# Sixteen products of the recurrence and a modulation part's products moved to GpSimd

## The chip, the cores and the metric

The kernel runs on one core of one Trainium2 chip. The metric is the device time of one execution in microseconds (us); lower is better. A core has five engines that work side by side: TensorE (PE in the profile), VectorE (DVE), ScalarE (ACT), GpSimd (POOL) and SyncE (SP, which here only issues DMAs). Each engine works through its own list of instructions in a fixed order, and an instruction that waits holds up everything behind it in that list.

## The reference

One decoder block over 512 positions of 1024 features, in fp32. What matters here:

```python
# six vectors of modulation, from the condition c
mod = silu(c) @ w_ada + b_ada            # shift1, scale1, gate1, shift2, scale2, gate2
h = rms_norm(x) * (1 + scale1) + shift1
xr, gr, q, k, v, gm = split(h @ w_in)
# branch A: recurrence
log_a = -8 * r * softplus(-lam);  a = exp(log_a)      # r, i: sigmoid gates of conv(xr)
u = sqrt(-expm1(2 * log_a)) * (i * xr)
hs_t = a_t * hs_(t-1) + u_t                            # along the positions
y_rnn = hs * gelu(gr)
# branch B: differential attention of q, k, v -> y_attn
x = x + gate1 * ((gate_a * (y_rnn @ w_proj_rnn) + gate_b * (y_attn @ w_proj_attn)) @ w_out)
h2 = rms_norm(x) * (1 + scale2) + shift2
out = x + gate2 * (relu(h2 @ w_ff1) ** 2 @ w_ff2)
```

## The kernel before

Activations lie with the features on 128 partitions and the 512 positions along a row: eight tiles of 128x512 make one 512x1024 matrix. Every matmul of a weight is done three times in a reduced fp32 format (`mm3`): the weight `w` is split into a high part `wh` (ScalarE, line 122) and a rest `wl` (VectorE, line 123), the activation likewise into a pair. So one 128x1024 weight unit costs a DMA of 512 KB, a cast on ScalarE, a subtraction on VectorE, and 24 matmuls of 512 columns. The loaded tiles `w` have three buffers in one pool, the pairs `wh`/`wl` two.

The program is written as one long list; a scheduler sorts it at build time into a fixed order for each engine. Around the change there are two places.

**The recurrence beside the first attention heads.** For each of the eight tiles n: `lru_sqrt` (a square root on ScalarE, line 453, then a product `xc<-xc,th` on VectorE, line 455), `lru_scan` (an exponential on ScalarE, line 460, then on VectorE line 461 and the scan of line 462), and `y_rnn` (product with the gate `gel` on VectorE, line 471; cast to `yh` on ScalarE, line 473; rest `yl` on VectorE, line 143). All these work in place in the tile `xc`. The string `PLAN` sets where the eight scans s0 to s7 stand between matmuls of the merge gates (`gm`) and of q and k (`qk`), and `heads()` interleaves them with the attention of the first two heads: scores `sc` (TensorE, line 582), their minimum and mask (VectorE, line 587, tile `e`), exponential (ScalarE, line 589), combination of the two maps (VectorE, line 596), transposes `aT` (TensorE, line 604), copies `aTs` (ScalarE line 607 or VectorE line 609), products with v, `po` (TensorE, line 615). When a head is done, `head_norm` scales its output `o` (VectorE, line 635) and `head_out` transposes it, `yT` (TensorE, line 642).

**The last modulation part (gate2).** It is a product of a 1024x1024 matrix with one vector, done by rows in eight pieces of 128x1024: load `ada` (a tile of the same pool and tag as the weights, three buffers), and one VectorE instruction (line 188) that multiplies by the vector `cb` and sums along the row. The eight pieces stand in the hidden-layer loops of the second and third quarter of the feed-forward net, after tiles n = 4 to 7 of each; each loop step also loads a weight of `w_ff1` (24 matmuls `f`), and applies relu and square on ScalarE (lines 865 and 876).

```python
if qd in (1, 2) and n >= 4:
    ada_chunk(5, 4 * (qd - 1) + n - 4)
```

Of the kernel before, what the change touches and what calls it, by code (L numbers as in the profile page):

```python
# [16 lines left out]
F32 = mybir.dt.float32  # L17
# [3 lines left out]
AF = mybir.ActivationFunctionType  # L21
ALU = mybir.AluOpType
AX = mybir.AxisListType

P = 128
S = 512
D = 1024
# [26 lines left out]
def build(tc, out, x, xT_in, c, pos, vecs, reps, ada, w_xr, w_xr7, w_qk, w_v, w_gr, w_gm, w_lru,  # L54
          w_pr, w_pa, w_out, w_ff1, w_ff2):
    nc = tc.nc
    from contextlib import ExitStack

    with ExitStack() as es:
        const = es.enter_context(tc.tile_pool(name="const", bufs=1))  # L60
        wpool = es.enter_context(tc.tile_pool(name="w", bufs=3))
# [9 lines left out]
        def slot(tag, bufs, name, dt=F32):  # L71
            return (big if tag in "mh" else mix).tile([P, S], dt, name=name, tag=tag, bufs=bufs)

        def t_(name, dt=F32, tag="t"):
            return (tmp if tag == "t" else mix).tile([P, S], dt, name=name, tag=tag,
                                                     bufs=dict(t=B_T, a=B_A, r=B_R)[tag])

        def tiny(name, n, dt=F32):
            return tmp.tile([P, n], dt, name=name, tag=f"s{n}", bufs=4 if n >= 32 else 12)
# [22 lines left out]
        def after(later, earlier):  # L102

            tc.add_manual_dep(later.ins, earlier.ins.name,
                              mybir.DependencyInfo(mybir.DependencyClass.NoSync, mybir.DependencyReason.DATA),
                              reason="activation tables")
# [35 lines left out]
        def split_l(dst, src, h):  # L142
            return nc.vector.tensor_tensor(dst, src, f32(h), op=ALU.subtract)
# [24 lines left out]
        cb = const.tile([P, D], F32, name="cb")  # L168
# [8 lines left out]
        bada = const.tile([P, 48], F32, name="bada")  # L177
# [4 lines left out]
        mod = const.tile([P, 48], F32, name="mod")  # L182

        def ada_chunk(j, k):
            col = j * 8 + k
            w = wpool.tile([P, D], F32, name=f"ada{col}", tag="w", bufs=3)
            nc.sync.dma_start(w, ada[j, k])
            nc.vector.tensor_tensor_reduce(w, w, cb, 1.0, bada[:, col:col + 1], op0=ALU.mult,  # L188
                                           op1=ALU.add, accum_out=mod[:, col:col + 1])

        def ada_halves(j, k, prev=None):

            col = j * 8 + k
            start = bada[:, col:col + 1]
            for i in range(2):
                w = slot("q", B_Q, f"ada{col}_{i}")
                cols = slice(i * S, (i + 1) * S)
                nc.sync.dma_start(w, ada[j, k][:, cols])
                end = mod[:, col:col + 1] if i else tiny(f"adah{col}", 1)
                i_ = nc.vector.tensor_tensor_reduce(w, w, cb[:, cols], 1.0, start, op0=ALU.mult,  # L200
                                                    op1=ALU.add, accum_out=end)
                start = end
                if prev is not None:
                    after(i_, prev)
# [247 lines left out]
        def lru_sqrt(n, u, th, prev):  # L452
            i = nc.scalar.activation(th, th, AF.Sqrt)
            after(i, prev)
            nc.vector.tensor_tensor(u, u, th, op=ALU.mult)
            return i

        def lru_scan(n, a, u, prev):
# [9 lines left out]
            return g, nc.scalar.activation(g, ps, AF.Gelu_apprx_tanh)  # L468

        def y_rnn(n, hs, g):  # L470
            nc.vector.tensor_tensor(hs, hs, g, op=ALU.mult)
            yh = slot("y", B_Y, f"yh{n}", F32R)
            nc.scalar.copy(yh, hs)
            yl = slot("y", B_Y, f"yl{n}", F32R)
            split_l(yl, hs, yh)
            return yh, yl
# [190 lines left out]
        for n in range(KC):  # L667
# [6 lines left out]
            if n == QT0:  # L674
                qk0 = qk_transpose(0, qk0)
        v0 = run(gv)
        sqs = [lru_sqrt(n, lg[n][1], lg[n][2], lg[-1][3]) for n in range(KC)]
        y_att = [None] * NH
        th0, m0, th1 = [], [], []
# [16 lines left out]
        def fill():  # L696

            rot = {}
            for group in PLAN.split("/"):
                for op in group.split():  # L700
                    o, n = op[0], int(op[1:])
                    if o == "g":
                        gate0(n)
                    elif o == "s":
                        hs = lru_scan(n, lg[n][0], lg[n][1], sqs[-1])
                        yr.append(y_rnn(n, hs, gel[n][0]))
                    elif o == "q":
                        rot[n] = yield from qk_quarter(n)
                    elif o == "t":
                        qks[n] = qk_transpose(n, rot.pop(n))  # L710
                    elif o == "v":
                        vs[n] = yield from v_half(n)
                    elif o == "p":
                        proj_rnn(n)
                    elif o == "m":
                        th1.append(gate(KC + n, slot("y", B_Y, f"thg{KC + n}")))
                if o not in "qv":
                    yield
# [49 lines left out]
        for n in range(KC):  # L768
            pp = project(w_pa[n], y_att, f"pa{n}")
            ada_chunk(3, n)  # L770
            th = t_(f"mg{n}")
            nc.vector.scalar_tensor_tensor(th, th1[n], 1.0, pp, op0=ALU.add, op1=ALU.mult)
            nc.vector.tensor_tensor(th, th, m0[n], op=ALU.add)
            mh = slot("y", B_Y, f"mh{n}", F32R)
            nc.scalar.copy(mh, th)
            ml = slot("q", B_Q, f"ml{n}", F32R)
            split_l(ml, th, mh)
            mg.append((mh, ml))
# [80 lines left out]
        def hidden_relu(qd, n, dst):  # L859
            if qd == 0 and n < NU:  # L860
                nc.vector.tensor_tensor(dst, early[n], rb2, op=ALU.mult)
                nc.scalar.activation(dst, dst, AF.Relu, bias=shw[:, n:n + 1])
            else:
                ps = project(w_ff1[qd, n], h2, f"f1_{qd}_{n}")
                nc.scalar.activation(dst, ps, AF.Relu)

        def hidden(qd, ahead):

            raw = [ff.tile([P, 4, S], F32, name=f"r2_{qd}_{c}", tag="raw", bufs=2) for c in range(2)]
            for n in range(KC):  # L870
                rl = raw[n // 4][:, n % 4, :]
                if n < len(ahead):
                    nc.scalar.activation(rl, ahead[n], AF.Square)
                else:
                    hidden_relu(qd, n, rl)
                    nc.scalar.activation(rl, rl, AF.Square)
                if qd in (1, 2) and n >= 4:
                    ada_chunk(5, 4 * (qd - 1) + n - 4)
            return raw

        def out_product(qd, raw, beside):
# [178 lines left out]
        for qd in range(4):  # L1060
            raw = hidden(qd, ahead)
            ahead = []

            def beside():

                if qd < 3:
                    ahead.append(t_(f"ahead{qd + 1}_{len(ahead)}"))
                    hidden_relu(qd + 1, len(ahead) - 1, ahead[-1])

            beside()  # L1070
            out_product(qd, raw, beside)
# [66 lines left out]
```

## Time and profile before

| | |
|---|---|
| median of 3 runs | 877.34 us (877.32 to 877.82) |
| the profiled execution's own time | 876.41 us |
| its span, first to last instruction | 874.6 us |
| TensorE busy | 861.0 us, 98% |
| VectorE busy | 651.5 us, 74% |
| ScalarE busy | 449.2 us, 51% |
| GpSimd busy | 15.1 us, 2% |
| granted TensorE clock | full in all 40 slices |

The span is 1.8 us shorter than the time of the execution it comes from, and that execution was 0.9 us below the median. "Busy" counts the time in which an engine has an instruction in work. Matmuls are pipelined and their recorded ends are modelled: two matmuls of 512 columns that follow each other start some 0.23 us apart, though each is listed with 0.39 us. So what TensorE loses is seen from the starts.

### The profile page before, as it was taken

The page shows a single profiled execution, that of the slowest core. Times are in us where ns is not written, and L with a number is a line of the kernel's source. Part 1 is how long each engine was busy: PE and PEld are TensorE (multiplying, and loading weights), DVE is VectorE, ACT ScalarE, POOL GpSimd, SP SyncE. Part 2 cuts the span into 40 slices and gives each one's busy share as a digit, 9 for nine tenths or more (in the row PEclk, how much of TensorE's full clock was granted, in tenths as well). Part 3 has the DMA queues.
Part 4 walks back from the last instruction along what each step waited for, and adds up shares of the span by engine and source line. Part 5 has one row for each costly group of instructions (what it writes and reads, how often), then busy time and mean ns, then how long its engine had stood idle before and what let it go on. Part 6 is the DMA issues. An engine that isn't in the chain of part 4 may idle for free.

```text
span 874.6 us, 11292 instructions
## 1 busy us (share of the span) xinstructions
PE 861.0 (98%) x4012; PEld 705.5 (81%) x4012; DVE 651.5 (74%) x1251; ACT 449.2 (51%) x748; POOL 15.1 (2%) x50
## 2 busy tenths in 40 slices
PE   6999999999999999999999999999999999999998
PEld 3888887877878888888888888888888888888887
DVE  6997995599859855786758556858766885876397
ACT  6673547985536543535623343747545544554461
POOL 1000000000000000000000000000000000002110
PEclk9999999999999999999999999999999999999999
DMA  8979425412255372238336332822641344139572
GB/s 315 370 250 319 152 97 134 136 68 73 87 131 169 99 191 76 93 87 227 110 126 210 132 121 75 273 87 72 193 148 70 128 161 169 49 126 235 120 122 96
DMA packets 64572, 128.92 MB, mean 147 GB/s; under 512 B 6146, under 2 KB 30850, under 8 KB 64516
## 3 DMA queue, kind: packets, MB, share of 16 engines
q1 hardware_dynamic: 59236, 122.97, 43.3%
q0 software_dynamic: 5280, 5.24, 3.9%
q8 instruction: 31, 0.51, 0.2%
q14 instruction: 25, 0.20, 0.1%
HBM read 113.51 MB, written 2.10 MB: 132 GB/s over the span
## 4 chain that ended last, share of the span: by engine, by line
PE 86%; DVE 10%; DMA 1%; issue 1%; ACT 1%; SPq 1%; ACTq 0%; DVEq 0%
PE f L131 6%; PE f L129 6%; PE f L130 6%; PE X L131 3%; PE X L130 3%; PE X L129 3%; PE gm L129 3%; PE gm L130 3%; PE gm L131 3%; DVE wl L123 2%; PE sc L582 2%; PE qk L131 2%; PE qk L129 2%; PE qk L130 2%; PE xr L129 2%; PE pr L129 2%
## 5 line engine op out<-in xcount | busy, mean ns | idle before, releaser
L122 ACT CAST wh<-w 128x1024 fp32r<-128x1024 f32 (+1 forms) x113 | 118.0, 1044 | 214.5 <-issue 48.1
L123 DVE TENSOR_TENSOR wl<-w,wh 128x1024 fp32r<-128x1024 f32 (+1 forms) x113 | 137.0, 1213 | 68.1 <-ACT wh L122 64.5
L131 PE MATMUL f<-h2h,wl 128*128 128x512 f32 x240 | 93.5, 390 | 0.4 <-DVE wl L123 0.4
L130 PE MATMUL f<-h2l,wh 128*128 128x512 f32 x240 | 93.2, 389 | 0.0
L129 PE MATMUL f<-h2h,wh 128*128 128x512 f32 x240 | 92.9, 390 | 0.0
L131 PEld LDWEIGHTS f<-h2h,wl 128*128 128x128 f32 x240 | 45.0, 188 | 10.1 <-DVE wl L123 0.8
L130 PEld LDWEIGHTS f<-h2l,wh 128*128 128x128 f32 x240 | 45.1, 188 | 9.4
L129 PEld LDWEIGHTS f<-h2h,wh 128*128 128x128 f32 x240 | 45.0, 188 | 9.3
L130 PE MATMUL gm<-hl,wh 128*128 128x512 f32 x128 | 51.0, 398 | 0.0
L129 PE MATMUL qk<-wh,hh 128*128 128x512 f32 x128 | 50.7, 396 | 0.0
L129 PE MATMUL gm<-hh,wh 128*128 128x512 f32 x128 | 50.5, 394 | 0.0
L131 PE MATMUL gm<-hh,wl 128*128 128x512 f32 x128 | 50.5, 394 | 0.0
L131 PE MATMUL qk<-wh,hl 128*128 128x512 f32 x128 | 50.4, 394 | 0.0
L130 PE MATMUL qk<-wl,hh 128*128 128x512 f32 x128 | 50.4, 394 | 0.0
L941 DVE TENSOR_TENSOR p_1l<-b,p_1h 128x1024 fp32r<-128x1024 f32 x24 | 29.4, 1223 | 26.3 <-ACT p_1h L940 26.1
L589 ACT ACTIVATE e<-e,nm 128x128 f32<-128x128 f32 (+3 forms) x64 | 35.7, 559 | 24.4 <-DVE nm L587 24.4
L940 ACT CAST p_1h<-b 128x1024 fp32r<-128x1024 f32 x24 | 25.2, 1051 | 31.0 <-PE f L130 22.9
L941 DVE TENSOR_TENSOR p_0l<-b,p_0h 128x1024 fp32r<-128x1024 f32 x24 | 29.3, 1223 | 15.0 <-ACT p_0h L940 13.8
L587 DVE CUSTOM_DVE_ANT_0 e<-sc,mask 128x128 f32<-128x128 f32 (+3 forms) x64 | 30.3, 484 | 9.9 <-PE sc L582 9.9
L940 ACT CAST p_0h<-b 128x1024 fp32r<-128x1024 f32 x24 | 25.3, 1055 | 24.2 <-PE X L131 12.4
L188 DVE CUSTOM_DVE_ANT_0 ada<-ada,cb,bada 128x1024 f32<-128x1024 f32 x16 | 20.5, 1283 | 14.3 <-DMA ada<-in_ada 14.1
L984 DVE TENSOR_TENSOR b<-b,b 128x1024 f32<-128x1024 f32 x24 | 29.1, 1220 | 0.1
(444 smaller groups left out, 2216.9 us busy)
## 6 DMA issues: line engine op xcount, KB each, us to landing
ada<-in_ada SPq DMA_DIRECT2D x64, 256.0 KB, 5.8
w<-in_w_ff SPq DMA_DIRECT2D x32, 512.0 KB, 3.2
b<-in_w_ff SPq DMA_DIRECT2D x30, 512.0 KB, 3.4
w<-in_w_qk SPq DMA_DIRECT2D x16, 512.0 KB, 3.2
w<-in_w_gm SPq DMA_DIRECT2D x16, 512.0 KB, 3.7
ada<-in_ada SPq DMA_DIRECT2D x16, 512.0 KB, 3.3
b_t<-in_w_ff POOLq DMA_DIRECT2D x10, 512.0 KB, 6.5
w<-in_w_gr SPq DMA_DIRECT2D x8, 512.0 KB, 4.0
```

Of the source, the lines that this page charges most:

```text
L122: i_w = nc.scalar.copy(wh[:, :n], w[:, :n])
L123: nc.vector.tensor_tensor(wl[:, :n], w[:, :n], f32(wh)[:, :n], op=ALU.subtract)
L129: nc.tensor.matmul(ps, lh, rh, start=first, stop=False, skip_group_check=more)
L130: nc.tensor.matmul(ps, lh, rl, start=False, stop=False, skip_group_check=more)
L131: nc.tensor.matmul(ps, ll, rh, start=False, stop=last, skip_group_check=more)
L188: nc.vector.tensor_tensor_reduce(w, w, cb, 1.0, bada[:, col:col + 1], op0=ALU.mult, op1=ALU.add, accum_out=mod[:, col:col + 1])
L582: nc.tensor.matmul(ps[m][:, :nn], q[m][:, qc], k[m][r][:, :nn], start=r == 0, stop=r == 1)
L587: nc.vector.tensor_tensor_reduce(e[:, :n], ps[m][:, :n], mask[:, S - n:], 1.0, 1e30, op0=ALU.add, op1=ALU.min, accum_out=nm)
L589: nc.scalar.activation(e[:, :n], e[:, :n], AF.Exp, bias=nm, scale=-1.0, accum_out=sums[:, m:m + 1])
L940: nc.scalar.copy(v4(wh), v)
L941: nc.vector.tensor_tensor(v4(wl), v, f32(v4(wh)), op=ALU.subtract)
L984: nc.vector.tensor_tensor(d, d, s_, op=ALU.add)
```

## The change

`lru_sqrt` and `y_rnn` issue their products on GpSimd instead of VectorE: 8 + 8 instructions of 128x512. The eight pieces of the last modulation part go through a new function: GpSimd multiplies (128x1024), ScalarE copies the product onto itself and sums it along the row, VectorE adds the bias to that one column. What is computed stays the same. Lines below 188 move down by 10 in the new kernel (471 becomes 481).

```diff
+        def ada_beside(j, k):
+
+            col = j * 8 + k
+            w = wpool.tile([P, D], F32, name=f"ada{col}", tag="w", bufs=3)
+            nc.sync.dma_start(w, ada[j, k])
+            nc.gpsimd.tensor_tensor(w, w, cb, op=ALU.mult)
+            sm = tiny(f"adas{col}", 1)
+            nc.scalar.activation(w, w, AF.Copy, accum_out=sm)
+            nc.vector.tensor_tensor(mod[:, col:col + 1], sm, bada[:, col:col + 1], op=ALU.add)
...
         def lru_sqrt(n, u, th, prev):
             i = nc.scalar.activation(th, th, AF.Sqrt)
             after(i, prev)
-            nc.vector.tensor_tensor(u, u, th, op=ALU.mult)
+            nc.gpsimd.tensor_tensor(u, u, th, op=ALU.mult)
             return i
...
         def y_rnn(n, hs, g):
-            nc.vector.tensor_tensor(hs, hs, g, op=ALU.mult)
+            nc.gpsimd.tensor_tensor(hs, hs, g, op=ALU.mult)
             yh = slot("y", B_Y, f"yh{n}", F32R)
             nc.scalar.copy(yh, hs)
...
                 if qd in (1, 2) and n >= 4:
-                    ada_chunk(5, 4 * (qd - 1) + n - 4)
+                    ada_beside(5, 4 * (qd - 1) + n - 4)
```

The scheduler sorts all engines anew. TensorE has the same rows; its order differs in the stretch of the first two heads. There, first before and then after, stand the rows around the transpose `yT` of head 0's output `o` (the `qk` are matmuls of q and k, `sc_3` the scores of head 1's last block of rows, `aT_1` a transpose of its second):

```order
L131 MATMUL qk_3_2105<-wh_2172,hl_298 128x512
L129 MATMUL qk_3_2105<-wh_2172,hh_346 128x512
L130 MATMUL qk_3_2105<-wl_2173,hh_346 128x512
L131 MATMUL qk_3_2105<-wh_2172,hl_350 128x512
L582 MATMUL sc_3_0_2203<-kh_3_0_1509,qs_1_0_1494 128x512
L582 MATMUL sc_3_0_2203<-kl_3_0_1512,qs_1_0_1494 128x512
L582 MATMUL sc_3_1_2204<-kh_3_1_1515,qs_1_1_1497 128x512
L582 MATMUL sc_3_1_2204<-kl_3_1_1518,qs_1_1_1497 128x512
L129 MATMUL qk_0_2102<-wh_2229,hh_398 128x512
L642 MATMUL yT_2156<-ident,o_2015 128x128 x4
```

```order
L131 MATMUL qk_3_2105<-wh_2172,hl_298 128x512
L652 MATMUL yT_2156<-ident,o_2015 128x128 x4
L129 MATMUL qk_3_2105<-wh_2172,hh_346 128x512
L130 MATMUL qk_3_2105<-wl_2173,hh_346 128x512
L131 MATMUL qk_3_2105<-wh_2172,hl_350 128x512
L592 MATMUL sc_3_0_2203<-kh_3_0_1509,qs_1_0_1494 128x512
L592 MATMUL sc_3_0_2203<-kl_3_0_1512,qs_1_0_1494 128x512
L592 MATMUL sc_3_1_2204<-kh_3_1_1515,qs_1_1_1497 128x512
L592 MATMUL sc_3_1_2204<-kl_3_1_1518,qs_1_1_1497 128x512
L129 MATMUL qk_0_2102<-wh_2229,hh_398 128x512
L614 MATMUL aT_1_2165<-ident,e_1_0_2087 128x128 x2
```

The transposes `yT` now stand eight matmuls of 512 columns further ahead.

On VectorE, at the same place, the rows that end with `o`, first before and then after (`xc_1247`, `xc_1292` and `xc_1337` are tiles 5, 6 and 7 of the recurrence, the `or` columns the scale of `o`, `cc` a column of the softmax; the scans, line 462, are listed with the name of their sibling instruction):

```order
L462 SCALAR_TENSOR_TENSOR xc_1247<-r_1650,xc_1247 128x512
L98 SCALAR_TENSOR_TENSOR or0b_2045<-or0a_2043,or0v 128x4
L461 SCALAR_TENSOR_TENSOR xc_1292<-r_1699,xc_1292 128x512
L99 SCALAR_TENSOR_TENSOR or_2026<-or0b_2045,or0y_2040 128x4
L593 RECIPROCAL rr_2050<-sm_2_2137 128x2
L471 TENSOR_TENSOR xc_1247<-xc_1247,gel_1245 128x512
L633 TENSOR_TENSOR or_2026<-or_2026,rr_1749 128x4
L595 SCALAR_TENSOR_TENSOR cc_2_2153<-sm_2_2137,nlam,rr_2050 128x1
L635 TENSOR_TENSOR o_2015<-o_2015,or_2026 128x512
```

```order
L98 SCALAR_TENSOR_TENSOR or0b_2045<-or0a_2043,or0v 128x4
L472 SCALAR_TENSOR_TENSOR xc_1337<-r_1718,xc_1337 128x512
L99 SCALAR_TENSOR_TENSOR or_2026<-or0b_2045,or0y_2040 128x4
L603 RECIPROCAL rr_2050<-sm_2_2137 128x2
L643 TENSOR_TENSOR or_2026<-or_2026,rr_1749 128x4
L605 SCALAR_TENSOR_TENSOR cc_2_2153<-sm_2_2137,nlam,rr_2050 128x1
L645 TENSOR_TENSOR o_2015<-o_2015,or_2026 128x512
```

The products of line 471 are gone (six of them stood ahead of `o`), and the scans of tiles 6 and 7 and line 461 of tile 7, which came after `o`, now come ahead of it.

On ScalarE, in the hidden loop of the second quarter, the rows from the relu of tile 3, first before and then after (`wh` are the casts of the weights of the next tiles, `adas` the sums of the modulation):

```order
L865 ACTIVATE r_1_0_6209<-f_1_3_6220 128x512
L876 ACTIVATE r_1_0_6209<-r_1_0_6209 128x512
L925 CAST a11h_6430<-r_1_0_6209 128x512
L122 CAST wh_6321<-w_6319 128x1024
L865 ACTIVATE r_1_1_6210<-f_1_4_6253 128x512
L876 ACTIVATE r_1_1_6210<-r_1_1_6210 128x512
L122 CAST wh_6357<-w_6355 128x1024
```

```order
L875 ACTIVATE r_1_0_6209<-f_1_3_6220 128x512
L886 ACTIVATE r_1_0_6209<-r_1_0_6209 128x512
L935 CAST a11h_6442<-r_1_0_6209 128x512
L198 ACTIVATE ada_6358,adas_6361<-ada_6358 128x1024
L122 CAST wh_6327<-w_6325 128x1024
L875 ACTIVATE r_1_1_6210<-f_1_4_6253 128x512
L886 ACTIVATE r_1_1_6210<-r_1_1_6210 128x512
L198 ACTIVATE ada_6397,adas_6400<-ada_6397 128x1024
L122 CAST wh_6366<-w_6364 128x1024
```

Each sum, which waits for GpSimd, stands directly ahead of a cast of the next weight. The load of the next `ada` tile now waits for that sum, since it takes its buffer.

## Rows read from the trace of the kernel before

**Rows 1.** The page: the span, and busy time of each engine (us, share).

```profile
span 874.6 us, 11292 instructions
PE 861.0 (98%) x4012; PEld 705.5 (81%) x4012; DVE 651.5 (74%) x1251; ACT 449.2 (51%) x748; POOL 15.1 (2%) x50
```

**Rows 2.** Busy time by stretch: bounds, length, then each engine, clock, DMA.

```profile
164.00:178.00 14.00, 14.00 (x65) 11.34 (x65) 9.96 (x23) 13.84 (x24) 0.00 (x0) 1.00 0.21 76
178.00:222.00 44.00, 42.15 (x213) 33.93 (x213) 43.82 (x102) 29.28 (x67) 0.00 (x0) 1.00 0.19 65
...
560.00:860.00 300.00, 299.63 (x1322) 247.77 (x1321) 215.59 (x228) 155.24 (x194) 12.86 (x10) 1.00 0.46 131
```

**Rows 3.** Waits of TensorE: what waited for what, us in total, times, longest.

```profile
PE aT L604 <- DVE e L596: 1.5, 4, 0.7
```

**Rows 4.** Order of time, TensorE, 190 to 218: start, duration, instruction, [idle before].

```profile
191.18 0.52 PE L604 MATMUL aT<-ident,e 128*128 128x128 f32 x3 [0.66 <-DVE e L596]
...
207.72 0.39 PE L129 MATMUL qk<-wh,hh 128*128 128x512 f32 x1
207.95 0.39 PE L130 MATMUL qk<-wl,hh 128*128 128x512 f32 x1
...
210.08 0.66 PE L642 MATMUL yT<-ident,o 128*128 128x128 f32 x4 [0.38 <-DVE o L635]
...
217.97 0.63 PE L604 MATMUL aT<-ident,e 128*128 128x128 f32 x4 [0.19 <-DVE e L596]
```

**Rows 5.** Order of time, VectorE, 164 to 224.

```profile
181.28 0.69 DVE L471 TENSOR_TENSOR xc<-xc,gel 128x512 f32<-128x512 f32 x1
181.89 0.48 DVE L596 SCALAR_TENSOR_TENSOR e<-e,cc,e 128x256 f32<-128x256 f32 x1
...
209.34 0.68 DVE L635 TENSOR_TENSOR o<-o,or 128x512 f32<-128x512 f32 x1
209.95 0.60 DVE L596 SCALAR_TENSOR_TENSOR e<-e,cc,e 128x384 f32<-128x384 f32 x1
```

**Rows 6.** VectorE by line, 178 to 222: count, busy us, mean ns, idle before.

```profile
L462 DVE TENSOR_TENSOR_SCAN xc<-r,xc 128x512 f32<-128x512 f32 x8 | 9.7, 1210 | 0.0
L123 DVE TENSOR_TENSOR wl<-w,wh 128x1024 fp32r<-128x1024 f32 x6 | 7.3, 1216 | 0.0
...
L471 DVE TENSOR_TENSOR xc<-xc,gel 128x512 f32<-128x512 f32 x8 | 5.5, 684 | 0.0
L461 DVE SCALAR_TENSOR_TENSOR xc<-r,xc 128x512 f32<-128x512 f32 x8 | 5.4, 679 | 0.0
L143 DVE TENSOR_TENSOR yl<-xc,yh 128x512 fp32r<-128x512 f32 x7 | 4.8, 682 | 0.0
L596 DVE SCALAR_TENSOR_TENSOR e<-e,cc,e 128x256 f32<-128x256 f32 (+3 forms) x7 | 4.0, 569 | 0.0
```

**Rows 7.** VectorE by line, 165 to 230: the first eight products of the recurrence.

```profile
L455 DVE TENSOR_TENSOR xc<-xc,th 128x512 f32<-128x512 f32 x8 | 5.0, 686 | 1.9 <-ACT th L453 1.9
```

**Rows 8.** Order of time, GpSimd, start of the program and its first DMA.

```profile
1.02 0.29 POOL masks.py:199 TENSOR_SCALAR_AFFINE_SELECT ident<-ident 128x128 f32<-128x128 f32 x1
...
789.74 1.41 POOL L896 DMA_DIRECT2D b_t<-in_w_ff  x1 [786.82 <-DVE p_1l L941]
```

**Rows 9.** Order of time, all engines, hidden loop of the second quarter, 648 to 661.

```profile
648.64 1.29 DVE L188 CUSTOM_DVE_ANT_0 ada<-ada,cb,bada 128x1024 f32<-128x1024 f32 x1 [2.07 <-DMA ada<-in_ada]
...
649.96 0.33 SPq L187 DMA_DIRECT2D ada<-in_ada  x1
...
653.34 1.28 DVE L188 CUSTOM_DVE_ANT_0 ada<-ada,cb,bada 128x1024 f32<-128x1024 f32 x1 [1.33 <-DMA ada<-in_ada]
...
655.14 1.05 ACT L122 CAST wh<-w 128x1024 fp32r<-128x1024 f32 x1 [3.23 <-PE f L130]
...
656.23 1.23 DVE L123 TENSOR_TENSOR wl<-w,wh 128x1024 fp32r<-128x1024 f32 x1 [1.59 <-ACT wh L122]
```

**Rows 10.** Order of time, ScalarE, 655 to 662.

```profile
660.58 1.05 ACT L122 CAST wh<-w 128x1024 fp32r<-128x1024 f32 x1 [1.85 <-PE f L130]
```

**Rows 11.** ScalarE by line, 165 to 230: the read of a sum.

```profile
L589 ACT ACTIVATION_READ_ACCUMULATOR e<-e,nm 128x1 f32 x16 | 3.0, 188 | 0.0
```

## The prediction

> **What bounds the kernel now.** I read the page first: TensorE is busy for 861.0 of 874.6 us [rows 1], so a change elsewhere can only win back time in which TensorE waits. Then busy time by stretch, to see where that is [rows 2]. In the feed-forward part (560 to 860) TensorE is busy for 299.63 of 300 us: whatever VectorE is spared there is worth nothing. From 164 to 178 it is busy throughout, too. From 178 to 222, where the recurrence and the first heads share VectorE, VectorE is busy for 43.82 of 44 us and TensorE for 42.15: here TensorE waits for VectorE. The list of TensorE's waits names what it waits for: the combined softmax tile `e`, 1.5 us in four waits [rows 3]; the order of time adds the head output `o`, 0.38 us [rows 4]. So at most some 2 us of idle time can be won, a little more since recorded matmul ends are late. That is 0.2% of the kernel, about what a measurement of it can tell from no change.
>
> **First eight products (line 455).** They cost VectorE 5.0 us, and between them it waited 1.9 us for ScalarE's square roots [rows 7]; TensorE does not wait there. Taking them off VectorE is worth nothing; the cover is TensorE's full queue of gate matmuls from 164 to 178. On GpSimd they need a price. The trace has no product on GpSimd. Its nearest row of the same engine is a one-input instruction of 128x128 at 0.29 us [rows 8]; four times that is 1.16 us for 128x512 and eight times 2.3 us for 128x1024. The other end is VectorE's own 0.68 us [rows 7] (about 1.2 for 128x1024 [rows 6]). I take the GpSimd figures, as the engine's own. Eight products from 169.5 on then end at 178.8; the first is needed at 178.2, the others later, one by one, so by themselves they delay nothing.
>
> **Second eight products (line 471).** Each takes 0.61 us of VectorE's queue (181.28 to 181.89 [rows 5]). What counts is not their sum of 4.9 us but when VectorE delivers what TensorE waits for. I follow the output `o`, which ends at 209.95 [rows 5]. In the new order six products ahead of it are gone (-3.7), but two scans (+2.4, at 1.21 [rows 6]) and one line 461 (+0.6) have moved ahead of it: `o` comes 0.7 us earlier, at 209.25. TensorE starts `yT` 0.13 us after `o` (210.08 [rows 4]), so at 209.4. But in its new list `yT` stands eight matmuls of 512 columns further ahead, and these take 0.23 us each (207.72 to 207.95 [rows 4]), 1.84 us, now to be done behind it. TensorE stands at that point at 209.4 + 1.84 = 211.2 instead of 210.1: a loss of 1.1 us, in which all earlier waits are contained, since `yT` waits either way. The later wait of 0.19 us at 217.97 [rows 4] goes. So +0.9.
>
> There is a new wait too. `yh` on ScalarE now waits for GpSimd, and behind it in ScalarE's list stand `aTs` and the exponentials of the head. After the second scan (ends about 183.5) GpSimd's product lasts to 184.7, `yh` to 185.2, and `aTs`, for which TensorE's `po` waits, to 185.5, where now it is done at 185.0. VectorE's `yl` and the next reciprocal wait behind the same `yh`. I put 0.5 us on VectorE for it: +1.4 for the stretch, if GpSimd and VectorE work side by side undisturbed.
>
> **Whether they do is the largest term, and no row shows it.** GpSimd is idle for 786.82 us before its first DMA [rows 8]; there is no instant with a product on both engines. Lower end: nothing. Upper end: while GpSimd reads its two operands, a VectorE instruction with two operands in SBUF waits to its end. The scans, `wl`, line 461, `yl` and the combination of `e` are such instructions: 9.7 + 7.3 + 5.4 + 4.8 + 4.0 = 31.2 us [rows 6] of the 38.3 that VectorE has left there (43.82 less 5.5), 81%. A product then costs VectorE up to 0.81 x 1.16 = 0.94 us, more than the 0.61 it took there itself. Nine stand ahead of `o`: the last two of line 455 (by 178.8) and seven of line 471. That is 0 to 8.5 us. No row is near either end, so I take the middle, 4.2.
>
> The Trainium skill speaks for the upper end: SBUF — State Buffer, section "Who interferes with whom", says that a VectorE instruction with two SBUF inputs contends with a GpSimd instruction that reads SBUF, and that one of them blocks until the other has finished. No run so far shows it here; by that rule the sum would have 8.5 for this term.
>
> **The modulation part.** VectorE is spared 8 x 1.28 us where TensorE never waits: worth 0. ScalarE gets eight sums (1.05 us like its cast of the same size [rows 9], and a read of the sum that adds some 0.1, half of 0.19 beside the copy [rows 11]), GpSimd eight products. The price lies in the chain through the three buffers. Now: the third `ada` of the quarter lands at 648.6, its VectorE instruction frees the buffer, the next load is issued at 649.96 and lands at 653.34, 3.4 later [rows 9]. After: 648.6 + 2.3 (GpSimd) + 1.15 (ScalarE) = 652.1; load, 655.5; GpSimd, 657.8; ScalarE, 658.9. Behind that sum in ScalarE's list stands the cast of tile 7's weight, which now starts at 655.14: it would end at 660.0, and `wl` (1.23 [rows 9]) at 661.2. TensorE begins that tile when it has finished the one before, about 660.6 (when the next cast gets its buffer [rows 10]), and needs `wl` two matmuls later, at 661.1. So the slack of 3.7 us (`wl` now ends at 657.4) is just used up: 0.1 us of stall, and each 0.1 us on GpSimd's price adds 0.2. In the other quarter, by the same count, some 1.5 us are left. Without disturbance: +0.2. Upper end: if the first `ada` product makes the `wl` due at that moment wait its 2.3 us, the load behind that `wl` and the next `ada` slip by about 1.6, and tile 7 stalls by some 1.4 us in each quarter: +2.9. Middle: +1.2, since TensorE's cover is thin here, not gone. (DMAs: the same eight loads, on the same queue; one weight load in each quarter is issued behind a sum instead of a VectorE instruction, 2 us later at most, and has several us to land.)
>
> **Sum.** +1.4 + 4.2 + 1.2 = +6.8 us on the profiled execution's 876.41: 883.2. The median stands 0.93 above that execution: **884.1 us**.
>
> **Rivals.**
> *A, side by side.* GpSimd and VectorE do not disturb each other. For it: VectorE and ScalarE show no such effect on each other in these rows. Against it: nothing in the trace. Sum +1.4 + 0.2: 878.9; with the small terms 877.5 to 880.
> *B, one at a time.* Each two-operand VectorE instruction waits for the whole GpSimd product. +1.4 + 8.5 + 2.9 = +12.8: 890.1. This is the skill page's rule, worked out with this kernel's rows. For it: 81% of VectorE's remaining work is of that kind, and VectorE has no idle time to absorb it. Against it: products that run while VectorE waits for ScalarE cost nothing.
> *C, the relief arrives (faster).* VectorE gets through its queue so much earlier that TensorE's 2 us of waits vanish: 877.34 - 2 = 875.3. It decides from the point where `o` is ready before 208.2, 1.0 us earlier than the count gives. Against it: the two scans ahead of `o`, whose 2.4 us are certain, and the transposes that moved ahead. For it: the count follows one wait; if the schedule's other shifts win more there than I see, the sign turns.
>
> **How the numbers follow.** The forecast, disturbance in part (+3 to +10): 0.38. B (+10 to +14): 0.27. A: 0.26, of which 0.19 lies within 0.2% (1.75 us) and 0.06 above, 0.01 below. C: 0.09, 0.06 of it faster by more than 0.2%. So faster 0.07, same 0.22, slower 0.71. The range runs from A's lower end into B: 877.6 to 891.0 leaves out C and the edge of A (0.10) below, and the upper part of B (0.09) above.
>
> **What would show it.** Right: TensorE's waits for `e` and `o` between 178 and 222 grow beyond 1.9 us; scans, line 461 and `yl` on VectorE are longer than 1210, 679 and 682 ns or start with gaps while GpSimd is busy; ScalarE's `yh` waits for GpSimd; feed-forward TensorE is busy for less than 299.63 of 300 us, just ahead of tile 7. GpSimd's products take about 1.2 and 2.3 us. A: VectorE's durations are unchanged, and TensorE loses about 1 us at `yT`. Wrong: TensorE reaches `yT` and does not wait, or GpSimd's price is far from 1.16, which enters nine times in one place and twice in the other.

## The result and the profile after

The changed kernel takes 890.60 us (median, 890.22 to 891.11) against 877.33 us before: ratio 1.0151, 95% interval 1.0135 to 1.0167, or 13.3 us slower (11.8 to 14.7). The profiled execution took 890.22 us with a span of 888.4 us, 13.8 us more than that of before [rows 1].

The page of the changed kernel, first lines:

```profile
span 888.4 us, 11319 instructions
PE 864.6 (97%) x4012; PEld 707.9 (80%) x4012; DVE 651.2 (73%) x1227; ACT 457.8 (52%) x764; POOL 59.2 (7%) x74
```

VectorE has 24 instructions fewer and is hardly less busy than before (651.2 against 651.5 us): its busy time has swallowed something. Busy time by stretch of the changed kernel (bounds, length, TensorE, its weight loads, VectorE, ScalarE, GpSimd, granted clock, DMA share, GB/s):

```profile
164.00:178.00 14.00, 14.00 (x65) 11.12 (x63) 6.09 (x13) 13.84 (x25) 8.06 (x6) 1.00 0.23 77
178.00:222.00 44.00, 33.27 (x153) 26.85 (x153) 41.46 (x84) 22.81 (x55) 16.82 (x11) 0.93 0.14 48
183.00:186.00 3.00, 0.32 (x3) 0.07 (x2) 3.00 (x5) 0.37 (x1) 1.75 (x1) 1.00 0.49 175
186.00:189.00 3.00, 2.22 (x10) 1.52 (x10) 2.54 (x6) 1.72 (x4) 1.65 (x1) 1.00 0.00 0
...
201.00:207.00 6.00, 6.00 (x28) 5.38 (x29) 6.00 (x12) 3.72 (x15) 2.17 (x1) 0.72 0.26 87
...
219.00:225.00 6.00, 5.37 (x25) 4.49 (x25) 4.59 (x8) 3.47 (x6) 0.00 (x0) 0.72 0.00 0
560.00:860.00 300.00, 299.11 (x1325) 246.87 (x1324) 213.03 (x224) 164.28 (x214) 32.12 (x18) 1.00 0.48 139
```

Against [rows 2], TensorE loses 8.9 us of busy time between 178 and 222 (42.15 to 33.27) and 0.5 in the feed-forward part (299.63 to 299.11). In 44 us VectorE now gets through 84 records of work, where it was 102. TensorE's waits from 164 to 245, what waited for what:

```profile
PE aT L614 <- DVE e L606: 5.7, 3, 2.7
PE yT L652 <- DVE o L645: 3.0, 1, 3.0
PE po L625 <- ACT aTs L617: 1.5, 1, 1.5
...
```

They are the same two names as in [rows 3, 4], `e` and `o`, with 8.7 us where there were 1.9, and `aTs`, which stands behind `yh` on ScalarE. Two of the long waits in the order of time, TensorE of the changed kernel:

```profile
200.96 0.63 PE L614 MATMUL aT<-ident,e 128*128 128x128 f32 x4 [2.60 <-DVE e L606]
...
219.63 1.12 PE L652 MATMUL yT<-ident,o 128*128 128x128 f32 x4 [2.95 <-DVE o L645]
```

What became of VectorE's instructions is seen in the order of time, GpSimd and VectorE of the changed kernel:

```profile
183.84 1.75 POOL L481 TENSOR_TENSOR xc<-xc,gel 128x512 f32<-128x512 f32 x1 [2.36 <-DVE xc L472]
196.34 3.93 POOL L481 TENSOR_TENSOR xc<-xc,gel 128x512 f32<-128x512 f32 x2 [7.61 <-DVE rr L603]
207.30 1.28 POOL L481 TENSOR_TENSOR xc<-xc,gel 128x512 f32<-128x512 f32 x1 [2.50 <-DVE xc L472]
```

```profile
172.62 2.20 DVE L123 TENSOR_TENSOR wl<-w,wh 128x1024 fp32r<-128x1024 f32 x1 [4.66 <-ACT wh L122]
...
180.25 2.32 DVE L123 TENSOR_TENSOR wl<-w,wh 128x1024 fp32r<-128x1024 f32 x1
...
183.79 0.68 DVE L471 SCALAR_TENSOR_TENSOR xc<-r,xc 128x512 f32<-128x512 f32 x1
184.40 1.48 DVE L606 SCALAR_TENSOR_TENSOR e<-e,cc,e 128x256 f32<-128x256 f32 x1
...
196.24 1.20 DVE L472 TENSOR_TENSOR_SCAN xc<-r,xc 128x512 f32<-128x512 f32 x1
197.36 1.18 DVE L605 SCALAR_TENSOR_TENSOR cc<-sm,nlam,rr 128x1 f32<-128x1 f32 x1
198.46 0.68 DVE L471 SCALAR_TENSOR_TENSOR xc<-r,xc 128x512 f32<-128x512 f32 x1
199.06 1.75 DVE L606 SCALAR_TENSOR_TENSOR e<-e,cc,e 128x512 f32<-128x512 f32 x1
...
218.90 0.68 DVE L645 TENSOR_TENSOR o<-o,or 128x512 f32<-128x512 f32 x1
```

How to read it: an `e` of 128x256 takes 0.48 us in [rows 5] and 1.48 here; `cc`, one column, 0.2 us elsewhere in the stretch, takes 1.18. They start while a product is on GpSimd, and the time of the wait is put into their own. It goes both ways: the product of 183.84 is issued while VectorE is in line 471 and takes 1.75 us where an unhindered one takes 1.28; the two of 196.34 take turns with the scan, `cc`, line 471 and `e`. VectorE's lengthened instructions ahead of `o`, from 177 us on, are ten: 0.6 + 0.4 + 1.1 + 1.0 + 1.0 + 1.0 + 0.7 + 0.9 + 1.1 + 1.1 = 8.9 us over their usual length, counted from their start to that of the next instruction. The first three (2.1 us) meet products with `th`, the other seven (6.8 us) products with `gel`.

In the feed-forward part, the same in another place (order of time, all engines, changed kernel):

```profile
652.68 2.41 POOL L196 TENSOR_TENSOR ada<-ada,cb 128x1024 f32<-128x1024 f32 x1 [25.75 <-DMA ada<-in_ada]
652.80 3.37 DVE L123 TENSOR_TENSOR wl<-w,wh 128x1024 fp32r<-128x1024 f32 x1
...
668.79 2.40 POOL L196 TENSOR_TENSOR ada<-ada,cb 128x1024 f32<-128x1024 f32 x1 [4.49 <-DMA ada<-in_ada]
...
671.22 1.06 ACT L198 ACTIVATE ada<-ada 128x1024 f32<-128x1024 f32 x1 [3.64 <-POOL ada L196]
...
672.28 1.03 ACT L122 CAST wh<-w 128x1024 fp32r<-128x1024 f32 x1
...
673.01 0.39 PE L131 MATMUL f<-h2h,wl 128*128 128x512 f32 x1
...
674.62 0.50 PE L131 MATMUL f<-h2h,wl 128*128 128x512 f32 x1 [0.53 <-DVE wl L123]
674.96 0.39 PE L129 MATMUL f<-h2h,wh 128*128 128x512 f32 x1
```

The second of the quarter's four products lengthens a `wl` from 1.23 to 3.37 us; the fourth comes late, its sum stands ahead of the cast of tile 7, and TensorE waits for that tile's `wl`. The listed wait of 0.53 us is not the whole loss: from the last matmul of tile 6 to the fourth of tile 7 the starts lie 1.95 us apart (673.01 to 674.96), where the same two lay 0.90 apart before (660.38 to 661.28), so 1.05 us are lost there.

### The profile page after: what moved, and what is told of

Its sections match the earlier page's. It is cut to its first block, busy times and chain, and to the rows that moved or that the text cites. A ratio compares the mean times of both kernels' runs of the same rounds, so it can differ in the third digit from the quotient of the medians.

```text
span 888.4 us, 11319 instructions
## 1 busy us (share of the span) xinstructions
PE 864.6 (97%) x4012; PEld 707.9 (80%) x4012; DVE 651.2 (73%) x1227; ACT 457.8 (52%) x764; POOL 59.2 (7%) x74
## 4 chain that ended last, share of the span: by engine, by line
PE 82%; DVE 10%; DMA 3%; issue 2%; ACT 1%; POOL 1%; SPq 0%; DVEq 0%; POOLq 0%; ACTq 0%
PE f L131 5%; PE f L129 5%; PE f L130 5%; PE X L130 3%; PE X L129 3%; PE X L131 3%; PE gm L130 3%; PE gm L129 3%; PE gm L131 3%; DVE wl L123 2%; PE qk L131 2%; PE qk L129 2%; PE qk L130 2%; DMA ada<-in_ada 2%; PE sc L592 2%; PE po L625 2%
## 5 line engine op out<-in xcount | busy, mean ns | idle before, releaser
L123 DVE TENSOR_TENSOR wl<-w,wh 128x1024 fp32r<-128x1024 f32 (+1 forms) x113 | 143.3, 1269 | 65.2 <-ACT wh L122 64.8
L196 POOL TENSOR_TENSOR ada<-ada,cb 128x1024 f32<-128x1024 f32 x8 | 19.2, 2399 | 514.9 <-DMA ada<-in_ada 453.1
```

What stands on the lines that cost most here:

```text
L123: nc.vector.tensor_tensor(wl[:, :n], w[:, :n], f32(wh)[:, :n], op=ALU.subtract)
L196: nc.gpsimd.tensor_tensor(w, w, cb, op=ALU.mult)
```

## The experiments

Three of them each do one part alone. In the first, TensorE's list is that of before; in the second, ScalarE's too; in the third it is that of the changed kernel. A difference in us is worked out from the ratio, which is taken against executions of the kernel before made beside that run (their medians lie between 877.19 and 877.59 us); it can be half a us off the difference of two medians.

**The modulation part alone** (against the changed kernel; both products back on VectorE):

```
-            nc.gpsimd.tensor_tensor(u, u, th, op=ALU.mult)
+            nc.vector.tensor_tensor(u, u, th, op=ALU.mult)
...
-            nc.gpsimd.tensor_tensor(hs, hs, g, op=ALU.mult)
+            nc.vector.tensor_tensor(hs, hs, g, op=ALU.mult)
```

> Only the modulation part's change (GpSimd product, ScalarE sum); all sixteen products of the recurrence stay on VectorE. TensorE's list of instructions is that of before. Theory (GpSimd and VectorE exclude each other, and the cost sits between 178 and 222 us): the stall of 0.5 us that the profile of the changed kernel shows at 670 to 680 us is all of it, so +0.5 us, 877.8 us. Rival (the modulation part costs the +1.2 us of the forecast, or more): 878.5 us or above. If neither the stall nor a loss is there: 877.3 us.

Measured: 879.48 us, ratio 1.0016 (1.0006 to 1.0025), +1.4 us. My theory had taken one profile's stall of 0.5 us for the whole; the rival's figure, that of the forecast, is the better one. The single times lie between 876.77 and 881.36 us, further apart than those of before (876.04 to 878.81). That the stall depends on when the loads land is my reading; no run shows it. In the profile of this run, whose execution was 1.5 us below its median, TensorE's starts lose about 0.6 us at tile 7 of the third quarter and 0.1 at that of the second.

**The eight products of `xc` and `th` alone** (against before):

```
-            nc.vector.tensor_tensor(u, u, th, op=ALU.mult)
+            nc.gpsimd.tensor_tensor(u, u, th, op=ALU.mult)
```

> Only the eight products of xc and th on GpSimd. Lists of TensorE and ScalarE are those of before, so a change of order can explain nothing. Theory (exclusion): the products run up to some 181 us, and each instruction of VectorE with two SBUF operands that meets one waits up to 1.2 us; two or three of them are on the way to the first heads' e: +1.5 to +3 us, 879 to 880.5 us. Rival (the order of instructions and the chain behind yh make the loss, not the meeting of engines): no change, 877.3 us.

Measured: 879.43 us, ratio 1.0023 (1.0014 to 1.0032), +2.0 us, as the theory has it. The lists of TensorE and ScalarE are those of before, and VectorE's differs by the eight products alone, so this is no matter of order. Its waits of TensorE (164 to 245):

```profile
PE aT L614 <- DVE e L606: 3.4, 5, 1.7
PE yT L652 <- DVE o L645: 0.4, 1, 0.4
```

The wait for `e` has gone from 1.5 to 3.4 us, about the whole loss. VectorE there:

```profile
178.03 0.96 DVE L606 SCALAR_TENSOR_TENSOR e<-e,cc,e 128x128 f32<-128x128 f32 x1
...
179.62 1.07 DVE L471 SCALAR_TENSOR_TENSOR xc<-r,xc 128x512 f32<-128x512 f32 x1
180.61 2.32 DVE L123 TENSOR_TENSOR wl<-w,wh 128x1024 fp32r<-128x1024 f32 x1
```

The three take 0.35, 0.68 and 1.22 us in the trace of before: 0.6 + 0.4 + 1.1 = 2.1 us, while the last products run on GpSimd, to 181.84.

**The eight products of `xc` and `gel` alone** (against before):

```
-            nc.vector.tensor_tensor(hs, hs, g, op=ALU.mult)
+            nc.gpsimd.tensor_tensor(hs, hs, g, op=ALU.mult)
```

> Only the eight products of xc and gel on GpSimd. TensorE's list is that of the changed kernel. Theory (exclusion, and a lower granted clock after the long waits): +8 to +10 us, 885 to 887 us, with GpSimd instructions of 1.3 to 2.2 us and VectorE's instructions of two SBUF operands longer by up to 1.2 us. Rival (order and chain alone, engines undisturbed): about +1.4 us, 878.7 us, with VectorE's durations as before.

Measured: 887.36 us, ratio 1.0108 (1.0095 to 1.0121), +9.5 us: far from the rival's 878.7, and just above the theory's 885 to 887. The three parts give 1.4 + 2.0 + 9.5 = 12.9 of 13.3 us. The order is not yet excluded here, since this list is the new one.

**Writes in place of products.** The changed kernel, with GpSimd only filling the tile that it multiplied (the factors are left out):

```
-            nc.gpsimd.tensor_tensor(u, u, th, op=ALU.mult)
+            nc.gpsimd.memset(u, 0.5)
...
-            nc.gpsimd.tensor_tensor(hs, hs, g, op=ALU.mult)
+            nc.gpsimd.memset(hs, 0.5)
```

> The changed kernel with each of the sixteen GpSimd products of the recurrence replaced by a GpSimd fill of the same tile with a constant (the factors th and gel are left out, so the output is another). TensorE's, VectorE's and ScalarE's lists are row for row those of the changed kernel; GpSimd only writes. Theory (reading of SBUF by GpSimd excludes VectorE's instructions of two SBUF operands): VectorE's durations are again 1.2 us for scans, 0.48 to 0.68 for e, and the time is before plus the order's share and the modulation's 0.5: 877.5 to 879.5 us. Rival 1 (the new order is the loss): 888 us or more, with long waits of TensorE for e and o at the same places. Rival 2 (writing alone also excludes): 882 us or more, VectorE's instructions lengthened by the fill's duration.

Measured: 879.52 us, ratio 1.0023 (1.0014 to 1.0031), +2.0 us. Of 13.3 us, 11 are gone, with every instruction of TensorE, VectorE and ScalarE in the same place in its list. The time lies at the upper edge of the theory's range, and both rivals miss it by more than 2 us. TensorE's waits there (164 to 245), and VectorE's `o` in the order of time:

```profile
PE aT L614 <- DVE e L606: 0.8, 2, 0.6
PE yT L652 <- DVE o L645: 0.7, 1, 0.7
PE po L625 <- ACT aTs L617: 0.4, 1, 0.4
PE sc L592 <- DVE nm L597: 0.3, 1, 0.3
```

```profile
209.46 0.69 DVE L645 TENSOR_TENSOR o<-o,or 128x512 f32<-128x512 f32 x1
```

`o` starts at 209.46, where it was 218.90 with products and 209.34 before. Since this kernel holds the modulation part too (+1.4), some 0.6 us are left for the new order; the two runs' intervals are wider than that, but TensorE's starts in the trace agree: they lie 0.9 us behind those of before at 165 us and 1.5 at the point that was at 222. A fill takes 0.53 us, not 1.28, so the chain behind `yh` is also shorter here; that part of the order's price is not separated, nor is that of the granted clock, 0.93 from 178 to 222 us in the changed kernel and 1.00 here. The first eight fills need no `th` and are over by 168.8 us, so only the later eight ran beside the full queue.

**Extra work on GpSimd beside the kernel before.** These three leave the sixteen products on VectorE and add eight GpSimd instructions, each into the gel tile that is no longer needed. No computation reads what they write, and the three share one list on each of the other engines.

```
             nc.vector.tensor_tensor(hs, hs, g, op=ALU.mult)
+            nc.gpsimd.tensor_tensor(g, hs, hs, op=ALU.mult)
```

> The kernel before, with all its products on VectorE, and eight GpSimd products more: after each product of xc and gel, GpSimd multiplies xc by itself into the gel tile that is no longer needed. Nothing computed waits for them; TensorE's list is that of before but for 12 rows of difference. Theory (exclusion): eight times up to 1.2 us on VectorE's full queue, +5 to +10 us, 882 to 887 us. Rival (no meeting cost, the loss was order and chain): 877.3 us, within 0.5.

Measured: 882.56 us, ratio 1.0064 (1.0051 to 1.0076), +5.6 us for work that nobody needs. Nothing is left of the rival.

```
             nc.vector.tensor_tensor(hs, hs, g, op=ALU.mult)
+            nc.gpsimd.tensor_scalar(g, hs, 2.0, None, op0=ALU.mult)
```

> As the run with extra products, but the extra GpSimd instruction multiplies xc by a constant: it reads one operand. The lists of TensorE, VectorE and ScalarE are the same as in that run. Theory (any GpSimd read of SBUF excludes VectorE's instructions of two SBUF operands): the loss is in the same proportion to the instruction's duration as there; if it takes about half as long, +2 to +5 us. Rival (only two operands on both sides exclude, or bandwidth is shared): less than a third of the loss there.

Measured: 879.57 us, ratio 1.0030 (1.0019 to 1.0041), +2.6 us: half of the loss, though the instruction is the longer one (1.49 us where nothing hinders it, against 1.04 for `xc` times itself). So my theory, that the loss goes by GpSimd's duration, is wrong; so is the rival's "less than a third". The same place in the two traces, with extra products first, then with one operand:

```profile
187.10 1.36 POOL L472 TENSOR_TENSOR gel<-xc 128x512 f32<-128x512 f32 x1 [3.96 <-DVE xc L471]
187.48 2.06 DVE L123 TENSOR_TENSOR wl<-w,wh 128x1024 fp32r<-128x1024 f32 x1
```

```profile
187.68 1.80 POOL L472 TENSOR_SCALAR gel<-xc 128x512 f32<-128x512 f32 x1 [3.08 <-DVE xc L471]
188.05 1.62 DVE L123 TENSOR_TENSOR wl<-w,wh 128x1024 fp32r<-128x1024 f32 x1
```

`wl`, 1.22 us long by itself, waits 0.84 us for the reading of two operands and 0.40 for that of one.

```
             nc.vector.tensor_tensor(hs, hs, g, op=ALU.mult)
+            nc.gpsimd.tensor_copy(g[:, :1], hs[:, :1])
+            nc.gpsimd.memset(g, 0.5)
```

> As the run with extra products, but the extra GpSimd work is a copy of one column of xc (which makes it wait at the same place) and then a fill of the whole tile, which reads nothing. Theory (reading excludes, writing does not): within 1 us of before, 877.3 to 878.3 us; VectorE's durations as before. Rival (writing excludes too): +2 us or more, in proportion to the fill's duration.

Measured: 877.40 us, ratio 1.0004 (0.9995 to 1.0013): no loss. A fill and the two-operand line 461 beside it (order of time):

```profile
181.91 0.68 DVE L461 SCALAR_TENSOR_TENSOR xc<-r,xc 128x512 f32<-128x512 f32 x1
182.10 0.53 POOL L473 MEMSET gel<- 128x512 f32 x1
```

Line 461 takes its 0.68 us as in [rows 6]. These fills disturb nothing; the instructions that read do.

**Relief that does not touch GpSimd** (against before):

```
-            if i % 2:
+            if i % 2 or hd < 2:
                 nc.scalar.copy(aT[:, :n], pt[:, :n])
```

> The kernel before, with the transposed weights of heads 0 and 1 all copied by ScalarE (line 609: four copies of 0.29 and 0.55 us between 178 and 222 us leave VectorE for ScalarE, which is busy for 29.28 of 44 us there). It touches no GpSimd. Theory (VectorE's queue there sets TensorE's waits of 1.9 us, and relief that costs nothing elsewhere is worth up to that): 875.5 to 877 us. Rival (the list of TensorE changes in 58 rows and gives it back, or the waits move to ScalarE): 877.3 us or above.

Measured: 877.63 us, ratio 1.0004 (0.9995 to 1.0013): nothing gained. TensorE waits 1.2 us for `o`, where it was 0.4, and less for `e`: in the new list the waits change places, as the rival says.

**Products cut in two** (against the run with the `gel` products alone):

```
-            nc.gpsimd.tensor_tensor(hs, hs, g, op=ALU.mult)
+            for q in (slice(0, S // 2), slice(S // 2, S)):
+                nc.gpsimd.tensor_tensor(hs[:, q], hs[:, q], g[:, q], op=ALU.mult)
```

> The run with only the eight products of xc and gel on GpSimd, each cut into two GpSimd instructions of 128x256; the lists of TensorE, VectorE and ScalarE are the same as in that run (887.4 us). Theory (exclusion instruction by instruction, so that two half products cost VectorE two half waits, and the second half waits in turn for a VectorE instruction in between): no gain, 886.5 to 889 us, VectorE's single waits about half as long but more of them, products later by up to a scan. Rival (VectorE waits for one instruction only, and slips in between the halves): about half of the loss, 882 to 884 us.

Measured: 887.50 us, ratio 1.0115 (1.0102 to 1.0128), +10.1 against +9.5 with whole ones; the intervals overlap. The first pair in the order of time:

```profile
181.75 2.01 POOL L482 TENSOR_TENSOR xc<-xc,gel 128x256 f32<-128x256 f32 x2 [178.82 <-DVE cc L606]
182.22 0.95 DVE L607 SCALAR_TENSOR_TENSOR e<-e,cc,e 128x256 f32<-128x256 f32 x1
183.10 1.74 DVE L472 TENSOR_TENSOR_SCAN xc<-r,xc 128x512 f32<-128x512 f32 x1
```

Two waits of half the length (0.47 in `e`, 0.53 in the scan) in place of one: smaller pieces buy nothing. A scan waits like the others.

**What the modulation part's loss hangs on** (against the first run above):

```
-            nc.gpsimd.tensor_tensor(w, w, cb, op=ALU.mult)
+            nc.vector.tensor_tensor(w, w, cb, op=ALU.mult)
```

> The modulation part alone, with its product on VectorE in place of GpSimd and its sum still on ScalarE, ahead of the same casts; TensorE's list is that of before, ScalarE's that of the run with the modulation part alone. Theory (the loss of that part, +1.4 us, hangs on GpSimd's 2.4 us in the chain of three buffers and on its meeting with wl): gone, 877.2 to 877.9 us. Rival (it hangs on ScalarE's sums ahead of the casts of the weights): it stays, 878.5 to 879.5 us.

Measured: 877.13 us, ratio 1.0002 (0.9994 to 1.0011). ScalarE's sums ahead of the casts cost nothing that can be measured; GpSimd's product does. Whether by its length in the chain of three buffers or by its meeting with `wl`, this run does not tell, as it takes away both.

**Where the first eight begin to cost** (against before):

```
-            nc.vector.tensor_tensor(u, u, th, op=ALU.mult)
+            (nc.gpsimd if n < 4 else nc.vector).tensor_tensor(u, u, th, op=ALU.mult)
```

> Only the first four of the eight products of xc and th on GpSimd, which run between 169 and 176 us, ahead of the first heads; the others stay on VectorE. TensorE's list is that of before. Theory (a meeting costs only where VectorE's queue sets TensorE's waits): they lengthen one or two wl there by up to 1 us, under TensorE's full queue: 877.0 to 877.8 us. Rival (each meeting costs, wherever): half of the loss of the eight, 878.2 to 878.6 us.

Measured: 878.90 us, ratio 1.0016 (1.0008 to 1.0025), +1.4 us. My theory falls. VectorE and TensorE there:

```profile
172.96 2.22 DVE L123 TENSOR_TENSOR wl<-w,wh 128x1024 fp32r<-128x1024 f32 x1 [4.65 <-ACT wh L122]
...
175.10 3.58 DVE L455 TENSOR_TENSOR xc<-xc,th 128x512 f32<-128x512 f32 x4
...
178.61 0.15 DVE L593 RECIPROCAL rr<-sm 128x2 f32<-128x2 f32 x1
...
179.50 0.44 PE L582 MATMUL sc<-kh,qs 128*128 128x384 f32 x1 [1.27 <-DVE nm L587]
```

`wl` is 1.0 us longer, the four VectorE products 1.1 (2.50 before). TensorE's full queue hides that only until the first head needs its reciprocal; ahead of that VectorE had 0.65 us of idle time in the trace of before, and 1.0 + 1.1 - 0.65 = 1.4 comes through. The rival's number was right; whether its reason was, the last run tells.

```
-            nc.vector.tensor_tensor(u, u, th, op=ALU.mult)
+            (nc.gpsimd if n < 2 else nc.vector).tensor_tensor(u, u, th, op=ALU.mult)
```

> Only the first two of the eight products of xc and th on GpSimd; all else as before, TensorE's list too. The run with the first four cost +1.4 us: its wl at 172.96 us waited 1.0 us, and VectorE's products behind it another 1.1, and only 0.65 us of that was slack. Theory (only meetings cost, there is no price for the use of GpSimd itself): the two products are done by about 173 us, before wl needs its operands or just as it starts; at most 0.3 us of wait, inside the slack: 877.0 to 877.6 us, and wl at that place is 1.2 to 1.5 us long. Rival (each product that leaves VectorE for GpSimd costs a share, wherever it runs): half of the loss of four, 877.9 us or more.

Measured: 877.71 us, ratio 1.0003 (0.9994 to 1.0012): no loss that can be measured. The time lies between the theory's range and the rival's, and the interval (-0.5 to +1.1 us) leaves room for the rival's +0.7; the trace does not: TensorE's waits from 164 to 245 us are those of before, 1.5 for `e` and 0.4 for `o`, where the run with four has 1.3 more. So the price is not a fixed one for each product. The place was another than expected:

```profile
171.35 2.56 DVE L455 TENSOR_TENSOR xc<-xc,th 128x512 f32<-128x512 f32 x2 [2.97 <-ACT th L453]
173.83 1.21 DVE L123 TENSOR_TENSOR wl<-w,wh 128x1024 fp32r<-128x1024 f32 x1
```

The meeting was with VectorE's own next two products (2.56 where two take 1.25), `wl` kept its length, and the slack hid the rest.

## Why the prediction came out as it did

The direction was right, and the range held the result, 0.4 us below its upper end. The likeliest case, 884.1 us, gave half of the loss; the measured time is that of rival B, 890.1 us, whose mechanism the runs show. That B's sum comes so near is in part luck: its +2.9 for the modulation part is 1.5 too much, and the 1.5 that TensorE's lower clock costs is not in it.

**What bounds the kernel**: right, as far as the runs go. The one attempt at TensorE's 2 us of waits, `aTs` on ScalarE, brought none of them back, and no version here beats the kernel before.

**Contention, +4.2**: this is the step that failed, and its sentence is "No row is near either end, so I take the middle". It measured 8.9 us on VectorE ahead of `o`, just over the upper end of 8.5 (which counted two products with `th` and seven with `gel`; there were three waits for the former and eight of the latter, of which seven cost a wait). The share of 81% was the wrong thing to multiply by: what counts is whether a two-operand instruction comes up at all while a product runs, and on a queue without a gap one nearly always does, however small. Four of the ten lengthened instructions are ones that the 81% did not count: `cc` of one column and three four-column steps of the norm. Of the `gel` products only that of 187.09 made no instruction wait, since VectorE was at the softmax step (line 597), which has its scores from PSUM, and then waited for ScalarE.

The Trainium skill (SBUF — State Buffer, "Who interferes with whom") says that a VectorE instruction with two SBUF inputs contends with a GpSimd instruction that reads SBUF and not with one that only writes. The runs agree on both: +5.6 us for extra products, none for extra fills. It also says (the same page, "Summary: rules for kernel authors") that the later of the two blocks until the earlier has finished. For two operands that is nearly so (0.84 us of a product of 1.04); for one operand `wl` waited 0.40 us of an instruction of 1.49, and there the measurement decides.

**First eight products, 0 by themselves**: wrong, +2.0. TensorE's full queue from 164 to 178 us was named as the cover, but the products ended at 181.5, not at 178.8: they started 0.4 later, their price of 1.28 adds 1.0, and they were held up themselves for 1.3. The `wl` at 172.62 waited 1.0 us at no cost, as VectorE then waited 2.1 us for ScalarE; the three instructions behind it, from 177 us on, had no such gap, and their 2.1 us are the loss. In the run with four products the cover was another, 0.65 us on VectorE's queue, since four products still stood there.

**Order and chain, +1.4**: the order's side is about 0.6 us by the run with writes (without the product's length). The new wait of `yh` was put at 0.5 us on VectorE and is 1.1 in the profile (0.87 for `yh` and 0.19 for the exponential behind it). `o` then comes out: 0.7 earlier by the new order (the forecast's count), 0.4 later at the start of the stretch, 8.9 and 1.1 later, 9.7 in all; the trace has 218.90 - 209.34 = 9.6.

**GpSimd's price**: 1.28 us against my 1.16, 2.40 against 2.3: right, from four and eight times the row of [rows 8]. There is luck in it: other GpSimd instructions of 128x512 took 0.53 (fill) to 1.49 us (product with a constant).

**The modulation part, +1.2**: +1.4 (0.5 to 2.2) in the run of its own. In the profile after, the loss (1.05) is at the place forecast, tile 7 of the second quarter, with what the forecast names: GpSimd's products follow one another at 6.9 us (661.92 to 668.79 in the profile after), as the forecast has their loads, a sum ahead of the cast, a `wl` that met a product (the second, where the forecast had the first). In the run of its own most of what its profile shows lies in the third quarter; where the rest of the median's +1.4 lies is not shown. The forecast's upper end does not follow from its own working: with some 1.5 us left in the other quarter, a slip of 1.6 stalls tile 7 there by 0.1, not by 1.4, which makes 1.8 in all and a middle of 1.0. So near a hit is in part luck.

**Not in the sum**: TensorE's clock. After the wait that ends at 200.96, and after that for `o`, which ends at 219.63, the granted clock over 6 us (201 to 207 and 219 to 225) is 0.72, a mean of a part at 1.2 GHz and a part at 2.4, where [rows 2] has 1.00 from 178 to 222. The first time hardly counts, since TensorE waits for `o` afterwards anyway; the second costs 5.37 x 0.28 = 1.5 us. The profile's 13.8 us are then: `o` 9.6, the eight matmuls that are now behind `yT` 1.84, the clock 1.5, the feed-forward part 1.05 by the starts, less the 0.19 of the old wait: 13.8. Each term is good to a few tenths; that they meet so exactly is chance.

## What to carry to other kernels

Work moved from VectorE to GpSimd is not taken off VectorE's queue if it reads SBUF, VectorE's other instructions have two operands there, and that queue has no gap: here a product of 0.61 us was exchanged for a wait of about 1 us, and a run with extra products beside the old kernel showed that in one step. Between two bounds, ask what would have to be true for each on a queue that is never empty, before taking the middle. And a cover has two ends: name what comes right behind it on the same queue, not only what hides it now.

## What was not expected of the hardware

- By the profile, whose spans on GpSimd are rough, its product with a constant (one operand) is slower, 1.49 us, than that of a tile with itself, 1.04; that of two tiles takes 1.28.
- The VectorE wait is about 0.4 us for each 512-column operand that GpSimd reads, in the two traces compared above (some 0.5 for a product of two tiles: 1.0 to 1.1 us), and not the length of GpSimd's instruction.
- Not every long wait of TensorE is followed by a lower clock: after 2.7 us that end at 185.93 the granted clock stays 1.00 (186 to 189 us above); after 2.6 and 3.0 us it is 0.72.
